# Three crossings of a decoder layer: rows scaled block by block, turned into four banks, with weight splits held behind the last norm

## The chip, the cores and the metric

The kernel runs on one core of one Trainium2 chip. The metric is the device time of one execution in microseconds (us); lower is better. Engines are named as in the profile: PE is TensorE's matmul, PEld its weight load, DVE is VectorE, ACT is ScalarE, POOL is GpSimd, SP is SyncE, whose queue issues most DMAs.

## What is computed

One layer of a hybrid decoder: 512 tokens of 1024 channels, all in float32. Every sub-layer stands between two RMS norms, and its normed output is added to the residual stream `h`.

```
h = x + 0.5 * post(SwiGLU_1(pre(x)))                   # FFN, 1024 -> 2816 -> 1024
u = pre(h);  proj = u @ W_in                           # queries, keys, gates, conv input
h = h + post((sigmoid(ga)*(dsa(...) @ Wa) + sigmoid(gb)*(conv(...) @ Wb)) @ W_out)
h = h + post(CrossAttn(pre(h), rms(mem)))              # 4 heads, 256 memory rows
h = h + 0.5 * post(SwiGLU_2(pre(h)))

def rms_norm(x, g):
    return x * rsqrt(mean(x*x, axis=-1) + 1e-6) * g
```

The branch `dsa` picks at most 128 keys per query by a score of its own and attends to them.

## The kernel before, in words

**Precision.** Each float32 operand is split into a high part (rounded by ACT to the type that PE multiplies fast) and a low part (the rest, subtracted on DVE). A product is three matmuls: high by high, high by low, low by high (`mm3`, `by_token`). Weights are split as they are needed: `Weights.prepare` rounds on ACT (line 146) and subtracts on DVE (line 147). `fetch` keeps `PIECES_AHEAD = 8` pieces of 512 columns split ahead of the unit in use; a unit of eight row blocks is two pieces. The raw tiles that the DMAs fill are six; one is free again when its low part has been taken.

**Two layouts.** The residual `h` and the outputs of the sub-layers lie by tokens: four blocks `t` of 128 tokens, each 1024 channels wide in two column halves `c`. The input `u` of the next sub-layer lies by channels: eight row blocks `k` of 128 channels, 512 tokens wide. `u` is a pair of high and low tiles.

**A crossing** is the way from one to the other. There are three: from the first FFN to the mixer, from the mixer to the cross-attention, from the cross-attention to the second FFN. Each does the following.

- `end` or `only` takes the product of one part `(c, t)` from PSUM, squares it on ACT with a running sum and multiplies it by the post gain on DVE.
- `settle(t)` takes the first norm's factor (a root on ACT and four small DVE steps, `inverse`), adds the scaled output to `h[t]` in two DVE instructions, squares these two halves on ACT and takes the second norm's factor `y`.
- `turned` scales the rows of two blocks by `y` on ACT into tiles `hn` and transposes them on PE, 16 transposes for half of the tokens, into four PSUM banks `pu`. Blocks `k` and `k + 1` lie next to each other in one bank.
- `gain_in` reads each block from PSUM, times the pre gain, and splits it into `u`: on ACT the high part, on DVE the low part. In the last crossing ACT first writes the float32 value (`us`, line 487) and then rounds it, and DVE subtracts from that.

In the first and the last crossing (`crossing`) PE goes on meanwhile with `head`, four weight units that start the next product for half of the tokens as soon as that half of `u` is there. The parts go in the order t outside, c inside. The first turn, of blocks 0 and 1, stands in the last part, ahead of its matmuls in the first crossing and ahead of its last two row blocks in the last one. The second turn stands between the third and the fourth head of the first half. In the middle crossing the products for the memory's keys (`pkx`) and values (`pvx`) lie around the turns.

**Order.** A planner orders the instructions of each engine by priority with its own estimates of durations, and each engine runs them in that order. `early(n)` raises the priority of what is written in its block; in a crossing PE keeps the order of the program. PSUM has eight banks: six go round under the tag `acc`, two under `aux`; `pu` takes two of each. Temporaries, `hn` and the squares among them, share ten tiles under the tag `ev`.

Of the kernel before, what the change touches and what calls it, by code (L numbers as in the profile page):

```python
# [9 lines left out]
F32 = mybir.dt.float32  # L10
F32R = mybir.dt.float32r
AF = mybir.ActivationFunctionType
ALU = mybir.AluOpType
# [3 lines left out]
P = 128  # L17
D = 1024
T = 512
NM = 256  # L20
KD = D // P
# [15 lines left out]
BEHIND, AHEAD, EVAC = 700, 400, 40  # L37
# [182 lines left out]
def build(tc, a, out):  # L220
    nc = tc.nc
    vec, ten = InOrder(tc, nc.vector), InOrder(tc, nc.tensor)
    ctx = ExitStack()
    with ctx:
# [21 lines left out]
        def ev(shape, dt, name):  # L246
            return evp.tile(shape, dt, tag="ev", name=name, bufs=EV)

        def bank(name):
            return acc.tile([P, 512], F32, tag="acc", name=name, bufs=ACC)  # L250

        def xbank(name, other=False):
            if other:
                return bank(name)
            return aux.tile([P, 512], F32, tag="aux", name=name, bufs=8 - ACC)

        def early(offset):
            return tc.high_priority(offset=offset)
# [6 lines left out]
        ident = con.tile([P, P], F32, name="ident")  # L265
# [5 lines left out]
        order = []  # L271
# [50 lines left out]
        def mm3(ps, wh, wl, xh, xl, first, last):  # L322
            ten.matmul(ps, wh, xh, start=first, stop=False)
            ten.matmul(ps, wh, xl, start=False, stop=False)
            ten.matmul(ps, wl, xh, start=False, stop=last)

        def product(ps, w, x, sl=FULL, ks=None):

            for k in range(len(w)) if ks is None else ks:
                (wh, wl), t = w[k], x[k]  # L330
                mm3(ps, wh, wl, t[0][:, sl], t[1][:, sl], k == 0, k == len(w) - 1)
# [43 lines left out]
        def new_u():  # L375
            return [pair("u") for _ in range(KD)]


        h = []
# [14 lines left out]
        class Outputs:  # L394
# [66 lines left out]
                    vec.scalar_tensor_tensor(o, o, y, h[t][:, cols], op0=ALU.mult, op1=ALU.add)  # L461
                    nc.sync.dma_start(out[t][:, cols], o)

            def turned(self, ys, n):

                hs = []
                for i in range(2):
                    t, y = 2 * n + i, ys[i]
                    hs.append([ev([P, T], F32, "hn") for _ in COLS])
                    for c, cols in enumerate(COLS):  # L470
                        nc.scalar.activation(hs[i][c], h[t][:, cols], AF.Copy, scale=y)
                pu = [xbank("pu", k2 % 2 == 1).rearrange("p (k t) -> p k t", k=2) for k2 in range(4)]
                for k in range(KD):
                    for i in range(2):
                        ten.transpose(pu[k // 2][:, k % 2, i * P:(i + 1) * P],
                                      hs[i][k // 4][:, k % 4 * P:(k % 4 + 1) * P], ident)
                return pu

            def gain_in(self, pu, n, pre, u, us=None):

                for k in range(KD):
                    ps, g, (uh, ul) = pu[k // 2][:, k % 2], gain(pre, k), (v[:, HALVES[n]] for v in u[k])
                    if us is None:
                        split_scaled(uh, ul, ps, g)
                        continue
                    w = us[k][:, HALVES[n]]
                    nc.scalar.activation(w, ps, AF.Copy, scale=g)
                    split(uh, ul, w)

        def crossing(outputs, part, pre, head, us=None):  # L490


            u, half = new_u(), [None, None]
            ten.on = True

            def turn(n):
                with early(AHEAD):
                    half[n] = outputs.turned(ys[2 * n:], n)
                    outputs.gain_in(half[n], n, pre, u, us)

            ys = []
            for t in range(T // P):
                for c in range(2):
                    if (c, t) == (1, 3):
                        part(c, t, lambda: turn(0))
                    else:
                        part(c, t)
                with early(AHEAD):
                    ys.append(outputs.settle(t))
            for f in head[:-1]:  # L510
                f(u, HALVES[0])
            turn(1)
            head[-1](u, HALVES[0])
            for f in head:
                f(u, HALVES[1])
            ten.on = False
            return u

        def heads(n, cols=()):
            ps = [bank("ph") for _ in range(n)]  # L520
            held, cols = {}, dict(cols)

            def make(i):
                def f(u, sl):
                    m = cols.get(i, P)
                    if i not in held:
                        held[i] = ws.unit(m)
                    product(ps[i][:m, sl], held[i], u, sl=sl)
                return f
            return ps, [make(i) for i in range(n)]  # L530

# [94 lines left out]
        def wide_units(n):  # L626
            return [w for _ in range(n) for w in ws.unit(T)]
# [76 lines left out]
        u = new_u()  # L704
        total, rows = sums_and_rows()
        ph, head = heads(4)
# [10 lines left out]
        outputs = Outputs("ffn1_post_g", 0.5)  # L717
        us = [slot([P, 2, T], F32, "us") for _ in range(4)]
        part = ffn(outputs, u, us, ph, rows, "ffn1_pre_g")
        load_h(a["xt"])  # L720
        ph, head = heads(4, {1: 72})
        u = crossing(outputs, part, "mix_pre_g", head)


        cs = slot([P, 2, T], F32, "cs")
# [37 lines left out]
        ps = ph[0]  # L763
# [9 lines left out]
        ps = xbank("pvt")  # L773
# [112 lines left out]
        for c in range(4):  # L886
            pg, pc = bank("pgc"), bank("pci")
            product(pg, ws.unit(), u)
            t = ev([P, T], F32, "gc")
# [6 lines left out]
            for k in (1, 0):  # L896
                o = 2 - k
                vec.scalar_tensor_tensor(s[:, o:], z[:, :T - o], convw[:, c, k:k + 1], s[:, o:],
                                               op0=ALU.mult, op1=ALU.add)
# [58 lines left out]
        for i in range(KD):  # L958
            t = ev([P, T], F32, "mt")[:, :NM]
# [3 lines left out]
        outputs = Outputs("mix_post_g", 1.0)  # L963
        for c in range(2):
            w = wide_units(KD // 2)
            for t in range(T // P):
                ps = bank("pf")
# [6 lines left out]
        for f in range(KD):  # L974
            ps = bank("pkx")[:, :NM]
            product(ps, ws.unit(), mn, sl=slice(0, NM))
            split(kx[f][:, 0], kx[f][:, 1], ps)
        u = new_u()
        for n in range(2):
            outputs.gain_in(outputs.turned([outputs.settle(t) for t in (2 * n, 2 * n + 1)], n), n, "xattn_pre_g", u)  # L980
        vx = [[None, None], [None, None]]
        for c in range(2):
            pv = [bank("pvx") for _ in range(2)]
# [12 lines left out]
        qx, at = [], []  # L996
# [54 lines left out]
        for f in range(KD):  # L1051
            ps = bank("pq")
# [7 lines left out]
        outputs = Outputs("xattn_post_g", 1.0)  # L1060
        w, pf = [wide_units(KD // 2)], []

        def partly(ts, ks):
            for t in ts:
                if t == len(pf):
                    pf.append(bank("pf"))
                tok = slice(t * P, (t + 1) * P)
                for k in ks:
                    (wh, wl), (xh, xl) = w[0][k], at[k]
                    ten.matmul(pf[t], xh[:, tok], wh, start=k == 0, stop=False)  # L1070
                    ten.matmul(pf[t], xh[:, tok], wl, start=False, stop=False)
                    ten.matmul(pf[t], xl[:, tok], wh, start=False, stop=k == KD - 1)
# [9 lines left out]
        def part(c, t, between=None):  # L1082
            if c == 0:
                partly((t,), range(6, 8))
                outputs.only(0, t, pf[t])
                return
            if len(w) == 1:
                w.append(wide_units(KD // 2))
            ps = bank("pf")
            by_token(ps, t, at, w[1], between and 6, between)  # L1090
            outputs.only(1, t, ps)

        ph, head = heads(4)
        uss = [slot([P, 2, T], F32, "us") for _ in range(4)]
        u = crossing(outputs, part, "ffn2_pre_g", head, [uss[k // 2][:, k % 2] for k in range(KD)])


        for t in range(T // P):
            nc.sync.dma_start(out[t], h[t])
        outputs = Outputs("ffn2_post_g", 0.5)  # L1100
        part = ffn(outputs, u, uss, ph)
# [72 lines left out]
```

## Time and profile before

| what | value |
|---|---|
| median of 3 runs (lowest to highest) | 1243.95 us (1243.83 to 1244.94) |
| the profiled execution's own time | 1246.46 us |
| its span, first to last instruction | 1244.7 us |
| PE busy | 1216.2 us, 98% |
| DVE busy | 845.9 us, 68% |
| ACT busy | 571.7 us, 46% |
| POOL busy | 78.9 us, 6% |
| HBM | 149.24 MB read, 4.19 MB written |

The profile is of one execution. Times in its views count from the first instruction, so they are to be held against the span. An engine's busy time is the time in which at least one of its instructions runs. The granted clock is given as a share of TensorE's full clock of 2.4 GHz; 0.5 would be 1.2 GHz, and what lies between is a mean over the stretch.

### The profile page before, as it was taken

The page shows a single profiled execution, that of the slowest core. Times are in us where ns is not written, and L with a number is a line of the kernel's source. Part 1 is how long each engine was busy: PE and PEld are TensorE (multiplying, and loading weights), DVE is VectorE, ACT ScalarE, POOL GpSimd, SP SyncE. Part 2 cuts the span into 40 slices and gives each one's busy share as a digit, 9 for nine tenths or more (in the row PEclk, how much of TensorE's full clock was granted, in tenths as well). Part 3 has the DMA queues.
Part 4 walks back from the last instruction along what each step waited for, and adds up shares of the span by engine and source line. Part 5 has one row for each costly group of instructions (what it writes and reads, how often), then busy time and mean ns, then how long its engine had stood idle before and what let it go on. Part 6 is the DMA issues. An engine that isn't in the chain of part 4 may idle for free.

```text
span 1244.7 us, 18396 instructions
## 1 busy us (share of the span) xinstructions
PE 1216.2 (98%) x7108; PEld 1077.1 (87%) x7108; DVE 845.9 (68%) x1493; ACT 571.7 (46%) x997; POOL 78.9 (6%) x118
## 2 busy tenths in 40 slices
PE   7999999999989999999999999999899999999997
PEld 7889999999879888888887898888788999999985
DVE  6877587767766799964357784555527567777665
ACT  6444443434454365455453583444825434344241
POOL 0000101110002300000000000000000111100100
PEclk9999999999989999999999999999899999999999
DMA  8336657564704642222222444233323556755641
GB/s 306 85 102 154 152 152 176 155 167 120 273 14 122 175 131 73 80 91 80 68 68 85 169 137 151 68 119 103 119 68 86 138 156 164 169 153 140 150 136 68
DMA packets 60904, 159.36 MB, mean 128 GB/s; under 512 B 7824, under 2 KB 10384, under 8 KB 60816
## 3 DMA queue, kind: packets, MB, share of 16 engines
q1 hardware_dynamic: 50320, 139.04, 34.7%
q0 software_dynamic: 10496, 19.14, 9.2%
q8 instruction: 56, 0.92, 0.3%
q14 instruction: 32, 0.26, 0.1%
HBM read 149.24 MB, written 4.19 MB: 123 GB/s over the span
## 4 chain that ended last, share of the span: by engine, by line
PE 89%; DVE 5%; ACT 3%; issue 1%; DMA 1%; SPq 0%; DVEq 0%; ACTq 0%
PE q L213 26%; PE pf L213 24%; PE pgb L213 4%; PE ph L213 4%; PE pa L213 4%; PE pq L213 4%; PE pga L213 4%; PE pb L213 3%; PE pkx L213 2%; PE pvx L213 2%; PE pya L213 2%; PE pyb L213 1%; PE pqb L213 1%; PE pqa L213 1%; PE pu L213 1%
## 5 line engine op out<-in xcount | busy, mean ns | idle before, releaser
L147 DVE TENSOR_TENSOR wl<-wraw,wh 128x1024 fp32r<-128x1024 f32 x246 | 294.0, 1218 | 116.4 <-ACT wh L146 101.6
L146 ACT CAST wh<-wraw 128x1024 fp32r<-128x1024 f32 x246 | 250.9, 1048 | 111.3 <-DVE wraw L163 87.7
L213 PE MATMUL q<-rt,wh 128*128 128x256 f32 x768 | 139.7, 283 | 0.0
L213 PEld LDWEIGHTS q<-rt,wh 128*128 128x128 f32 x768 | 119.8, 192 | 0.0
L126 POOL DMA_DIRECT2D wraw<-in_up x64 | 55.3, 915 | 962.6 <-DMA wraw<-in_up 749.7
L213 PE MATMUL q<-rt,wl 128*128 128x256 f32 x384 | 108.9, 284 | 0.0
L213 PE MATMUL pf<-wh,hidh 128*128 128x512 f32 x256 | 100.6, 393 | 0.0
L213 PE MATMUL pf<-wl,hidh 128*128 128x512 f32 x256 | 100.4, 392 | 0.0
L213 PE MATMUL pf<-wh,hidl 128*128 128x512 f32 x256 | 100.1, 391 | 0.0
L213 DVE TENSOR_TENSOR o<-o,q 128x512 f32<-128x512 f32 (+1 forms) x128 | 67.6, 548 | 10.6 <-PE q L213 8.3
L213 PEld LDWEIGHTS q<-rt,wl 128*128 128x128 f32 x384 | 73.7, 192 | 0.3 <-DVE wl L147 0.3
L213 PE MATMUL q<-u,wh 128*128 128x256 f32 x384 | 70.4, 283 | 0.0
L213 PE MATMUL q<-r,wh 128*128 128x256 f32 x384 | 70.4, 283 | 0.0
L213 PEld LDWEIGHTS q<-u,wh 128*128 128x128 f32 x384 | 60.9, 192 | 1.3
L213 PEld LDWEIGHTS q<-r,wh 128*128 128x128 f32 x384 | 60.9, 192 | 1.2
L213 PE MATMUL pf<-wh,hid 128*128 128x512 f32 x192 | 60.5, 390 | 0.0
L213 PE MATMUL pgb<-u,wh 128*128 128x512 f32 x192 | 59.3, 389 | 0.0
L213 PEld LDWEIGHTS pf<-wh,hidl 128*128 128x128 f32 x256 | 48.4, 189 | 10.3
L213 DVE TENSOR_TENSOR f<-f,pf 128x512 f32<-128x512 f32 x48 | 32.8, 683 | 35.7 <-PE pf L213 35.6
L213 PEld LDWEIGHTS pf<-wh,hidh 128*128 128x128 f32 x256 | 48.6, 190 | 9.5
L213 PEld LDWEIGHTS pf<-wl,hidh 128*128 128x128 f32 x256 | 48.5, 189 | 9.1
L315 ACT CAST hidh<-o 128x1024 fp32r<-128x1024 f32 x16 | 16.8, 1051 | 85.9 <-DVE o L213 85.9
(265 smaller groups left out, 2735.7 us busy)
## 6 DMA issues: line engine op xcount, KB each, us to landing
wraw<-in_up SPq DMA_DIRECT2D x55, 512.0 KB, 5.2
wraw<-in_up SPq DMA_DIRECT2D x98, 256.0 KB, 4.6
wraw<-in_down SPq DMA_DIRECT2D x44, 512.0 KB, 4.4
wraw<-in_w_in SPq DMA_DIRECT2D x37, 512.0 KB, 4.4
wraw<-in_up POOLq DMA_DIRECT2D x64, 256.0 KB, 5.6
wraw<-in_w_out SPq DMA_DIRECT2D x8, 512.0 KB, 3.7
wraw<-in_w_k SPq DMA_DIRECT2D x8, 512.0 KB, 4.4
wraw<-in_w_v SPq DMA_DIRECT2D x8, 512.0 KB, 4.5
```

Of the source, the lines that this page charges most:

```text
L126: self.nc.gpsimd.dma_start(t[:, o:o + PIECE], src, accum_op=ALU.add)
L146: self.nc.scalar.copy(hi, src)
L147: self.nc.vector.tensor_sub(lo, src, f32(hi))
L213: ins = f(*args, **kwargs)
L315: nc.scalar.copy(dst_h, src)
```

## The change

- `settle` and the scaling of a block become one step, `normed(t)`: the rows of block `t` are scaled as soon as its second norm is known, column half 0 on ACT, column half 1 on DVE. `turned` only transposes.
- The eight row blocks go over the four banks in turn: block `k` lies in bank `k % 4`, so blocks `k` and `k + 4` share one.
- In the first and the last crossing, DVE instructions that are written in the block of the heads, among them the low parts of the weights that follow, are ordered behind the DVE half of the last `hn` (`tc.issue_after(last.ins)`).
- The second turn moves from ahead of the fourth head to behind its sixth row block.
- The order of the parts becomes an argument; the last crossing now takes `PARTS`, c outside and t inside, with the first turn in the last part as before.

```diff
-            def turned(self, ys, n):
-                hs = []
-                for i in range(2):
-                    t, y = 2 * n + i, ys[i]
-                    hs.append([ev([P, T], F32, "hn") for _ in COLS])
-                    for c, cols in enumerate(COLS):
-                        nc.scalar.activation(hs[i][c], h[t][:, cols], AF.Copy, scale=y)
-                pu = [xbank("pu", k2 % 2 == 1).rearrange("p (k t) -> p k t", k=2) for k2 in range(4)]
+            def normed(self, t):
+                y = self.settle(t)
+                hn = [ev([P, T], F32, "hn") for _ in COLS]
+                nc.scalar.activation(hn[0], h[t][:, COLS[0]], AF.Copy, scale=y)
+                return hn, vec.tensor_scalar(hn[1], h[t][:, COLS[1]], y, None, op0=ALU.mult)
+
+            def turned(self, hs):
+                pu = [xbank("pu", b % 2 == 1).rearrange("p (k t) -> p k t", k=2) for b in range(4)]
+                pu = [pu[k % 4][:, k // 4] for k in range(KD)]
                 for k in range(KD):
                     for i in range(2):
-                        ten.transpose(pu[k // 2][:, k % 2, i * P:(i + 1) * P], ...)
+                        ten.transpose(pu[k][:, i * P:(i + 1) * P], ...)
...
-            ys = []
-            for t in range(T // P):
-                for c in range(2):
-                    if (c, t) == (1, 3):
-                        part(c, t, lambda: turn(0))
-                    else:
-                        part(c, t)
-                with early(AHEAD):
-                    ys.append(outputs.settle(t))
-            for f in head[:-1]:
-                f(u, HALVES[0])
-            turn(1)
-            head[-1](u, HALVES[0])
-            for f in head:
-                f(u, HALVES[1])
+            for c, t in order:
+                part(c, t, (lambda: turn(0)) if (c, t) == order[-1] else None)
+                if c == 1:
+                    with early(AHEAD):
+                        x, last = outputs.normed(t)
+                        hs.append(x)
+            with tc.issue_after(last.ins):
+                for f in head[:-1]:
+                    f(u, HALVES[0])
+                head[-1](u, HALVES[0], 6, lambda: turn(1))
+                for f in head:
+                    f(u, HALVES[1])
...
-        u = crossing(outputs, part, "mix_pre_g", head)
+        u = crossing(outputs, part, [(c, t) for t in range(4) for c in range(2)], "mix_pre_g", head)
...
-            outputs.gain_in(outputs.turned([outputs.settle(t) for t in (2 * n, 2 * n + 1)], n), n, "xattn_pre_g", u)
+            hs = [outputs.normed(t)[0] for t in (2 * n, 2 * n + 1)]
+            outputs.gain_in(outputs.turned(hs), n, "xattn_pre_g", u)
...
-        u = crossing(outputs, part, "ffn2_pre_g", head, [uss[k // 2][:, k % 2] for k in range(KD)])
+        u = crossing(outputs, part, PARTS, "ffn2_pre_g", head, [uss[k // 2][:, k % 2] for k in range(KD)])
```

## Rows read from the trace of the kernel before

**Rows 1.** The page's first part: busy time, share, instructions.

```profile
PE 1216.2 (98%) x7108; PEld 1077.1 (87%) x7108; DVE 845.9 (68%) x1493; ACT 571.7 (46%) x997; POOL 78.9 (6%) x118
```

**Rows 2.** Stretches of the span: each engine's busy time, granted clock, DMA share, GB/s.

```profile
355.95:368.40 12.45, 9.06 (x35) 7.68 (x35) 5.70 (x17) 8.84 (x20) 0.00 (x0) 0.73 0.00 0
...
711.30:760.10 48.80, 48.56 (x322) 44.50 (x321) 35.54 (x75) 35.72 (x73) 0.00 (x0) 1.00 0.50 162
873.70:878.50 4.80, 3.52 (x23) 2.97 (x23) 1.85 (x7) 4.78 (x12) 0.00 (x0) 1.00 0.10 42
878.50:888.30 9.80, 9.62 (x73) 8.80 (x71) 8.27 (x17) 7.44 (x16) 0.00 (x0) 1.00 0.26 81
888.30:898.30 10.00, 6.20 (x30) 6.00 (x30) 4.33 (x14) 8.96 (x24) 1.77 (x2) 0.66 0.73 216
...
440.00:540.00 100.00, 99.19 (x457) 81.09 (x456) 98.16 (x241) 53.97 (x108) 0.00 (x0) 1.00 0.29 92
```

**Rows 3.** PE's instructions in order: start, us, shape, count, [idle before, releaser].

```profile
358.60 0.33 PE L213 MATMUL pu<-ident,hn 128*128 128x128 f32 x1 [2.49 <-ACT hn L471]
359.82 3.46 PE L213 MATMUL pu<-ident,hn 128*128 128x128 f32 x15 [0.90 <-ACT hn L471]
...
378.12 0.33 PE L213 MATMUL pu<-ident,hn 128*128 128x128 f32 x1 [0.98 <-ACT hn L471]
379.80 3.29 PE L213 MATMUL pu<-ident,hn 128*128 128x128 f32 x15 [1.35 <-ACT hn L471]
...
874.22 0.33 PE L213 MATMUL pu<-ident,hn 128*128 128x128 f32 x1 [0.39 <-ACT hn L471]
875.44 1.86 PE L213 MATMUL pu<-ident,hn 128*128 128x128 f32 x15 [0.90 <-ACT hn L471]
877.05 0.48 PE L213 MATMUL pf<-wh,at 128*128 128x512 f32 x1
...
890.81 0.33 PE L213 MATMUL pu<-ident,hn 128*128 128x128 f32 x1 [2.50 <-ACT hn L471]
892.44 3.46 PE L213 MATMUL pu<-ident,hn 128*128 128x128 f32 x15 [1.30 <-ACT hn L471]
```

**Rows 4.** DVE's instructions in order of time.

```profile
350.72 0.35 DVE L213 SCALAR_TENSOR_TENSOR stat<-stat 128x1 f32<-128x1 f32 x2
...
362.30 0.88 DVE L213 SCALAR_TENSOR_TENSOR u<-pu,gains,u 128x256 fp32r<-128x256 f32 x2 [0.54 <-ACT u L319]
...
860.93 0.35 DVE L213 SCALAR_TENSOR_TENSOR stat<-stat 128x1 f32<-128x1 f32 x2
...
898.56 0.76 DVE L213 TENSOR_TENSOR u<-us,u 128x256 fp32r<-128x256 f32 x2 [0.58 <-ACT u L315]
```

**Rows 5.** ACT's instructions in order of time.

```profile
854.83 0.60 ACT L424 ACTIVATE sq<-pf 128x512 f32<-128x512 f32 x1 [0.97 <-PE pf L213]
...
881.34 0.64 ACT L424 ACTIVATE sq<-pf 128x512 f32<-128x512 f32 x1
...
893.38 0.84 ACT L487 ACTIVATE us<-pu,gains 128x256 f32<-128x256 f32 x2 [0.38 <-PE pu L213]
```

**Rows 6.** The chain that ended last, merged: start, length, instructions of a piece.

```profile
319.37 32.68 PE pf L213 x144
...
383.09 14.32 PE ph L213 x120
...
895.90 15.46 PE ph L213 x120
```

**Rows 7.** Groups by line: count, busy, mean ns of one, idle before.

```profile
L471 ACT ACTIVATE hn<-h,stat 128x512 f32<-128x512 f32 x24 | 15.9, 713 | 0.5 <-DVE stat L213 0.5
...
L147 DVE TENSOR_TENSOR wl<-wraw,wh 128x1024 fp32r<-128x1024 f32 x246 | 294.0, 1218 | 116.4 <-ACT wh L146 101.6 <-issue 11.3 <-DMA wraw<-in_up 2.1
L146 ACT CAST wh<-wraw 128x1024 fp32r<-128x1024 f32 x246 | 250.9, 1048 | 111.3 <-DVE wraw L163 87.7 <-PE q L213 12.0 <-DMA wraw<-in_up 9.6
```

**Rows 8.** The selection's replacements, a group by line.

```profile
L213 DVE MATCH_REPLACE8 bias<-m,bias 128x256 f32<-128x256 f32 (+2 forms) x48 | 25.7, 538 | 0.0
```

More of the change, by code (lines that the diff above doesn't have):

```diff
@@ L462, in settle_last @@
                     nc.sync.dma_start(out[t][:, cols], o)
-            def turned(self, ys, n):
-                hs = []
-                for i in range(2):
-                    t, y = 2 * n + i, ys[i]
-                    hs.append([ev([P, T], F32, "hn") for _ in COLS])
-                    for c, cols in enumerate(COLS):
-                        nc.scalar.activation(hs[i][c], h[t][:, cols], AF.Copy, scale=y)
-                pu = [xbank("pu", k2 % 2 == 1).rearrange("p (k t) -> p k t", k=2) for k2 in range(4)]
+            def normed(self, t):
[6 more added lines that the diff above has]
+                pu = [pu[k % 4][:, k // 4] for k in range(KD)]
                 for k in range(KD):
                     for i in range(2):
-                        ten.transpose(pu[k // 2][:, k % 2, i * P:(i + 1) * P],
-                                      hs[i][k // 4][:, k % 4 * P:(k % 4 + 1) * P], ident)
+                        ten.transpose(pu[k][:, i * P:(i + 1) * P], hs[i][k // 4][:, k % 4 * P:(k % 4 + 1) * P], ident)
                 return pu
             def gain_in(self, pu, n, pre, u, us=None):
-                for k in range(KD):
-                    ps, g, (uh, ul) = pu[k // 2][:, k % 2], gain(pre, k), (v[:, HALVES[n]] for v in u[k])
+                for k, ps in enumerate(pu):
+                    g, (uh, ul) = gain(pre, k), (v[:, HALVES[n]] for v in u[k])
                     if us is None:
@@ L488, in gain_in, with crossing @@
                     split(uh, ul, w)
-        def crossing(outputs, part, pre, head, us=None):
-            u, half = new_u(), [None, None]
+        def crossing(outputs, part, order, pre, head, us=None):
+            u, hs = new_u(), []
             ten.on = True
@@ L497, in turn @@
                 with early(AHEAD):
-                    half[n] = outputs.turned(ys[2 * n:], n)
-                    outputs.gain_in(half[n], n, pre, u, us)
-            ys = []
-            for t in range(T // P):
-                for c in range(2):
-                    if (c, t) == (1, 3):
-                        part(c, t, lambda: turn(0))
-                    else:
-                        part(c, t)
-                with early(AHEAD):
-                    ys.append(outputs.settle(t))
-            for f in head[:-1]:
-                f(u, HALVES[0])
-            turn(1)
-            head[-1](u, HALVES[0])
-            for f in head:
-                f(u, HALVES[1])
+                    outputs.gain_in(outputs.turned(hs[2 * n:]), n, pre, u, us)
+            for c, t in order:
[10 more added lines that the diff above has]
+                    f(u, HALVES[1])
             ten.on = False
@@ L523, in make, with f @@
             def make(i):
-                def f(u, sl):
+                def f(u, sl, at=None, between=None):
                     m = cols.get(i, P)
@@ L527, in f @@
                         held[i] = ws.unit(m)
-                    product(ps[i][:m, sl], held[i], u, sl=sl)
+                    if at:
+                        product(ps[i][:m, sl], held[i], u, sl=sl, ks=range(at))
+                        between()
+                    product(ps[i][:m, sl], held[i], u, sl=sl, ks=range(at or 0, KD))
                 return f
```

## The prediction

> **What bounds the kernel now.** The page's table of busy time says that TensorE (PE) is the bound [rows 1]: all that can be won by a change of order is its idle time and the stretches in which it runs below its full clock. I then cut the span at the three crossings, where the tokens' rows are normalized, turned and split for the next product [rows 2]. The reader is to see that the three differ. In the second (711.30 to 760.10) PE is busy 48.56 of 48.80 us, because the memory's keys and values fill it. In the first, the stretch 355.95 to 368.40 has 9.06 of 12.45 us busy at a mean granted clock of 0.73. In the third, 888.30 to 898.30 has 6.20 of 10.00 at 0.66. Last I went to PE's instructions in order of time for the waits themselves [rows 3]. Each crossing turns two halves of the tokens, 16 transposes each. Ahead of them PE waits 2.49 + 0.90, 0.98 + 1.35, 0.39 + 0.90 and 2.50 + 1.30 us, always for the scaled rows hn on ScalarE (ACT). After the long waits the 15 transposes take 3.46 us, after the short one of the third crossing 1.86.
>
> What sets these waits: all four activations hn of a half are written where the half is turned, so they stand on ACT behind the settling of later blocks. The second half has a slower cause: on VectorE (DVE) the small steps of the last norm alternate with the low parts of weights, 1.2 us each [rows 7]. An undisturbed block goes from its square at 854.83 to its last small step (860.93 + 0.35) in 6.45 us, with two instructions of another block in its way. The last block of the third crossing starts its square at 881.34 and its last 15 transposes wait until 892.44 [rows 3 to 5].
>
> **The price of PE's work at full clock.** A 512-column matmul of the last slab is 32.68 / 144 = 0.227 us, a 256-column one of the heads 14.32 / 120 = 0.1193 [rows 6]. Fifteen transposes fill 875.44 to 877.05, so one is 0.107 and 16 are 1.72 [rows 3]. The heads are 4 x 2 x 24 = 192 matmuls, 22.91 us; three of them serve one row block, 0.358.
>
> **First crossing, part by part.** Scaling as each norm ends: hn of blocks 0 and 1 exist some 4 us before 355.95 (block 1's last small step is at 350.72 [rows 4]), so the first turn starts at 355.95 without its 3.39 us of waits. Half of each hn moves to DVE: 713 ns on ACT today, and on DVE I take 0.5, nearer to that than to nothing, since DVE's low part of twice the elements is 1.2 [rows 7]. The eight pieces of a crossing cost PE nothing but behind the last norm, where one counts, as today: PE's parts hide the others, and without that cover each pair would cost at most 0.7. The turn itself keeps the full clock (16 x 0.107), because PE now comes to it out of unbroken matmuls. The last part's 18 matmuls follow (4.08), then three heads (8.59), 18 matmuls of the fourth (2.15), the second turn (1.72), the other 6 (0.72) and the second halves of four heads (11.45). The sum is 1.72 + 4.08 + 22.91 + 1.72 = 30.43 us against 397.41 - 355.95 = 41.46 today [rows 6].
>
> Now what can still be late. The last norm starts when the last part ends (361.75), with 0.7 for the add and 6.45 for the chain; 0.7 for hn and up to one high part of a weight on ACT (1.05 [rows 7]) give 369.6 to 370.7. PE comes to the second turn at 355.95 + 1.72 + 4.08 + 8.59 + 2.15 = 372.49. So no wait is left; this is what the move by 18 matmuls gives, beside the splits that stay behind. Those four low parts (1.2 us each) now run from about 370 to 375 on DVE. They belong to the units after the heads, since eight pieces ahead are already split when the crossing begins, so PE needs them only after 386. Behind them on DVE wait the low parts of u, behind these the first head's second half; on SP the four loads into the freed raw tiles, then cos and sin, needed only by DVE's rotations.
>
> The rotation of banks: today two neighbouring blocks share a bank, and DVE's next pair of low parts (0.88) waits 0.54 for ACT each time [rows 4], 0.71 per block; inside a pair the second adds 0.40. With blocks over four banks I take 0.40 throughout. Against this, a bank is complete only when its second block is in it: the first read comes after the tenth transpose instead of the fourth, 1.07 us into the turn. The first low part of u would then be ready at 372.49 + 1.07 + 0.2 + 0.48 + 0.48 = 374.7, the last at 377.5, while PE wants the last at 374.93 + 7 x 0.358 = 377.4. That is a stall of 0.1; with the weight splits still in DVE's way to 375, or with the norm half a microsecond late, 1 to 3. I take 1.2, nearer the low end, because only the last split overlaps. **First crossing: 41.46 - 30.43 - 1.2 = 9.8 us won** (8.0 to 10.9).
>
> The wait by bank rests on the 0.54 us rows: ACT and DVE wait for each other though they read different columns. The Trainium skill (PSUM — Partial Sum Buffer, "PSUM bank collisions raise a hardware error") states the same and speaks against the new layout: readers are to be kept off a bank, not off an address, while PE writes it. By that rule the read waits for ten transposes; by addresses alone for two, and the four turns would begin their reads 0.86 us sooner, of which the two second turns would show, some 1.7 us in all.
>
> **Third crossing.** The new order of parts puts four short ones (6 matmuls each) first, then four of 24, and the first turn stands 6 matmuls from the end; PE's amount is the same: 1.72 + 1.36 + 22.91 + 1.72 = 27.71 us, from 873.70. Today the heads end at 895.90 + 15.46 = 911.36, 37.66 later [rows 6]. Here each block of u costs ACT two instructions, and ACT alone reads the banks, so their rotation wins nothing. From the first of them (893.38) to the last low part (898.56 + 0.76) it is 5.94 us [rows 4, 5], where PE wants 2.87. Today 24 matmuls of cover hide that in the second half; with 6 left it shows. First half: reads begin at 873.70 + 1.07 + 0.2, with block 2's hn on ACT in between (0.65), so u ends at 881.56; PE wants its last block at 876.78 + 2.51 = 879.29, a stall of 2.27. The first head ends at 881.92, the second turn starts at 889.80 (two heads and 18 matmuls later). The last norm, whose square still waits for u's casts until about 881.4, needs 7.2 to 8.2 us more, ends by 889.6, and is hidden, if only just. Second half: u ends at 889.80 + 1.27 + 5.94 = 897.01, PE wants it at 894.75: again 2.26. The heads end at 873.70 + 27.71 + 4.53 = 905.94. **Third crossing: 5.4 us won** (4 to 6.3).
>
> **Second crossing.** ACT and DVE get the same edits, but PE idles only 0.24 us there [rows 2] and u is used 15 us after it is ready: nothing. Without the cover of the values' products, a wait for ten transposes instead of four would cost 0.65 twice.
>
> **The sum.** 9.8 + 5.4 = 15.2 us. The profiled execution took 1246.46 us (span 1244.70), so it would take 1231.2; the median of the runs is 2.51 lower, so 1243.95 - 15.2 = 1228.7.
>
> **The rivals.** (a) The clock falls all the same. Transposes, then matmuls with gaps of 0.3 us per block, replace idle time; the rows show 0.73 and 0.66 for stretches with waits of 2.5 us and transposes, but 1.00 for 873.70 to 878.50 with 1.29 us of waits and the same 16 transposes, and 1.00 for 878.50 to 888.30 with small gaps [rows 2]. At half clock a second turn costs 1.6 more (3.46 against 1.86) and its next 6 to 8 triples some 2: twice 3.6, giving 1235.9. (b) The high parts of those weights, which nothing holds back on ACT, get into the last norm: four of them are 4.2 us [rows 7], of which at most one was counted. Three more (3.1) put hn at 373.8 in the first crossing and at 892.7 in the third; the low parts behind it then hold u back by another 3 in the first. PE waits 1.3 + 3 - 1.2 and 2.9 longer: 6.0 in all, 1234.7. (c) The first crossing's gain is swallowed later. From 440 to 540 DVE is busy 98.16 of 100 us [rows 2]; if it, not PE, set the pace there, 9.8 would be lost: 1238.5. With (a) in the third crossing as well, 1242. Against it: DVE's work there starts from the heads' results and moves with them, and PE is busy 99.19. (d) Slower: the planner puts the selection, 48 replacements of 0.54 us [rows 8] with as many searches of about the same length, some 51 us, in one piece ahead of the weight splits of that stretch. Eight pieces ahead cover four units, 4 x 24 x 0.227 = 21.8 us of PE, so a piece over 21.8 + 15.2 = 37 us decides; all 51 us of it would give 1228.7 + 51 - 21.8 = 1257.9. (e) The change does not do what it says: the ten shared buffers hold hn back (eight are hn's, squares need the others), and the first turns wait as now: 3.4 and 1.3 us less gain, 1233.4.
>
> **How the numbers follow.** Forecast 60 in 100, with 1226 to 1232 as its own range; (a) 13, (b) 8, (e) 7, (c) 5, (c) with (a) 3, (d) 4. The range goes from 1225.5, the low bounds of both stalls plus 1.5, to 1237, which takes in (a), (b) and (e). More than 0.2% (2.5 us, about what a measurement of this kernel can tell from no change) faster: 0.93 less a little for mixtures, 0.92. Within it: 0.04, from (c) with (a) and mixtures. Slower: 0.04.
>
> **What would show it.** First turns with no wait for hn and 1.9 us long; second turns 18 matmuls into the fourth head, no wait, clock 1.00; on DVE four low parts of weights directly behind the last hn; in the third crossing the first head of each half stretched from 2.9 to about 5 us, waiting for u; the first crossing's heads over at 397.41 - 9.8 = 387.6, the third's at 911.36 - 15.2 = 896.2, with unchanged work behind both. Wrong it would be by a clock below 1.00 behind the turns, by a wait for hn, or by PE gaps between 440 and 540 that grow beyond 0.81.

## The result and the profile after

The changed kernel took 1232.01 us (median of 4 runs, 1231.74 to 1232.19) against 1244.37 (4 runs, 1243.83 to 1244.94): a ratio of 0.9900, 95% interval 0.9883 to 0.9918, 12.4 us less. The forecast was 1228.7 with a range of 1225.5 to 1237. The profiled execution took 1232.19 us, span 1230.4, mean granted clock 0.997.

The page's busy times answer to [rows 1]:

```profile
PE 1211.4 (98%) x7108; PEld 1073.4 (87%) x7108; DVE 851.4 (69%) x1505; ACT 564.8 (46%) x985; POOL 78.9 (6%) x118
```

The same matmuls are counted busy for 4.8 us less. That goes with the low clock that is gone from the turns: the transposes behind the long waits alone took 4.6 us more than at full clock (3.46 + 3.29 + 3.46 against 3 x 1.86 [rows 3]). Twelve halves of hn have gone from ACT to DVE.

PE's waits by what ended them (us in all, times, longest). Before, this line led the list:

```profile
PE pu L213 <- ACT hn L471: 10.8, 8, 2.5
```

No wait for hn is left:

```profile
PE ph L213 <- ACT whl L146: 7.1, 1, 7.1
PE po L213 <- ACT pth L315: 0.7, 3, 0.3
PE ph L213 <- ACT u L315: 0.7, 2, 0.4
PE ps_stat L213 <- DVE rows L213: 0.6, 1, 0.6
PE ph L213 <- DVE u L213: 0.6, 1, 0.6
```

The third and the fifth line are new, and they are a part of the stalls for u that the prediction priced. The list does not show all of a stall: where PE gets on in small steps, as each piece of u comes, only the starts of its instructions tell it. PE's instructions in order of time, to set beside [rows 3]:

```profile
356.85 1.91 PE L213 MATMUL pu<-ident,hn 128*128 128x128 f32 x16
...
373.44 1.91 PE L213 MATMUL pu<-ident,hn 128*128 128x128 f32 x16
...
864.11 1.91 PE L213 MATMUL pu<-ident,hn 128*128 128x128 f32 x16
867.82 0.85 PE L213 MATMUL ph<-u,wh 128*128 128x256 f32 x2 [0.41 <-ACT u L315]
869.76 1.00 PE L213 MATMUL ph<-u,wh 128*128 128x256 f32 x2 [0.25 <-ACT u L315]
...
881.88 1.91 PE L213 MATMUL pu<-ident,hn 128*128 128x128 f32 x16
```

All four turns run through in 1.91 us, without a wait. The stretches that answer to [rows 2] (length, then busy time of PE, PEld, DVE, ACT and POOL, granted clock, DMA share, GB/s):

```profile
355.90:368.40 12.50, 12.50 (x87) 11.50 (x87) 10.79 (x35) 7.84 (x23) 0.00 (x0) 1.00 0.00 0
702.10:750.50 48.40, 48.40 (x321) 44.39 (x321) 37.23 (x80) 33.46 (x69) 0.00 (x0) 1.00 0.51 163
863.00:867.80 4.80, 4.41 (x28) 3.55 (x26) 3.33 (x13) 2.61 (x10) 0.00 (x0) 1.00 0.27 111
867.80:874.00 6.20, 5.67 (x25) 4.83 (x26) 4.12 (x12) 6.20 (x17) 0.00 (x0) 0.72 0.00 0
874.00:881.90 7.90, 7.90 (x69) 7.90 (x68) 6.01 (x17) 5.26 (x11) 0.00 (x0) 1.00 0.22 75
881.90:889.00 7.10, 6.92 (x49) 6.09 (x48) 5.03 (x10) 6.03 (x18) 0.00 (x0) 1.00 0.86 271
431.00:531.00 100.00, 99.16 (x456) 81.02 (x455) 98.47 (x241) 53.91 (x108) 0.00 (x0) 1.00 0.30 91
```

The first crossing has lost its gap and its low clock (9.06 of 12.45 us at 0.73 before). The third keeps one stretch, 867.80 to 874.00, in which ACT never rests, PE waits for u, and the clock is 0.72. The long stretch behind the first crossing swallowed nothing.

DVE's instructions in order of time around the first crossing's second turn:

```profile
371.09 0.49 DVE L213 TENSOR_SCALAR hn<-h,stat 128x512 f32<-128x512 f32 x1
371.50 4.80 DVE L147 TENSOR_TENSOR wl<-wraw,wh 128x1024 fp32r<-128x1024 f32 x4
376.21 3.22 DVE L213 SCALAR_TENSOR_TENSOR u<-pu,gains,u 128x256 fp32r<-128x256 f32 x8
```

The last hn, then the four low parts of weights, then u: the order foreseen. The stall behind it is the 0.6 us wait of the list above. ACT's instructions in order of time in the third crossing, first half:

```profile
865.32 0.63 ACT L424 ACTIVATE sq<-h 128x512 f32<-128x512 f32 x1 [2.19 <-DVE h L213]
...
865.95 0.62 ACT L424 ACTIVATE sq<-h 128x512 f32<-128x512 f32 x1
...
866.56 0.45 ACT L489 ACTIVATE us<-pu,gains 128x256 f32<-128x256 f32 x1
...
867.97 0.73 ACT L469 ACTIVATE hn<-h,stat 128x512 f32<-128x512 f32 x1
```

Two squares of block 2 stand ahead of the first read of the turned block, and block 2's hn comes in between. The prediction counted this hn, not the squares.

**Where the time went.** Between the crossings the work is the same, so each can be measured as the distance between two products outside it: the first from the first start of pf<-wh,hidh to the first of pgc<-u,wh, the third from the first start of pq<-u,wh to the last of pa<-u,wh. The start of pf tells how long the part ahead of all edits took. In us, for the profiled execution of each kernel of this study, with the median of its runs:

| kernel | start of pf | first crossing | third crossing | both | median |
|---|---|---|---|---|---|
| before | 161.6 | 269.2 | 188.8 | 458.0 | 1244.37 |
| before, again | 162.2 | 266.5 | 187.8 | 454.3 | 1243.08 |
| changed | 162.5 | 259.5 | 184.1 | 443.6 | 1232.01 |
| changed, again | 162.2 | 259.7 | 184.1 | 443.8 | 1232.21 |
| rows scaled where turned | 162.8 | 264.1 | 185.1 | 449.2 | 1235.04 |
| early rows alone | 163.1 | 263.9 | 186.9 | 450.8 | 1239.98 |
| splits not held | 162.1 | 259.9 | 185.5 | 445.4 | 1233.88 |
| banks as before | 162.5 | 260.1 | 182.8 | 442.9 | 1231.39 |
| second turn ahead | 161.2 | 260.3 | 182.9 | 443.2 | 1230.45 |
| four blocks outside | 162.5 | 259.4 | 182.6 | 442.0 | 1230.57 |
| splits behind u | 162.7 | 258.8 | 184.3 | 443.1 | 1231.48 |
| and a turn sooner | 162.1 | 259.0 | 183.2 | 442.2 | 1230.17 |
| all three | 161.6 | 259.0 | 181.7 | 440.7 | 1228.81 |
| all three, by bank | 162.5 | 259.2 | 181.8 | 441.0 | 1229.74 |

The start alone scatters by 1.9 us, though nothing ahead of it differs in the source; a difference of medians below that has to be looked for in the crossings.

### The profile page after: what moved, and what is told of

The parts are those of the page before. It is cut to its first block, busy times and chain, and to the rows that moved or that the text cites. A ratio compares the mean times of both kernels' runs of the same rounds, so it can differ in the third digit from the quotient of the medians.

```text
span 1230.4 us, 18394 instructions
## 1 busy us (share of the span) xinstructions
PE 1211.4 (98%) x7108; PEld 1073.4 (87%) x7108; DVE 851.4 (69%) x1505; ACT 564.8 (46%) x985; POOL 78.9 (6%) x118
## 4 chain that ended last, share of the span: by engine, by line
PE 86%; DVE 7%; ACT 3%; DMA 1%; issue 1%; SPq 0%; DVEq 0%; ACTq 0%
PE q L213 26%; PE pf L213 20%; PE ph L213 5%; PE pgb L213 4%; PE pa L213 4%; PE pq L213 4%; PE pga L213 4%; PE pb L213 4%; PE pkx L213 2%; PE pvx L213 2%; PE pya L213 2%; DVE f L213 2%; ACT sq L424 1%; PE pyb L213 1%; PE pqb L213 1%; PE pqa L213 1%
```

## The experiments

Each time goes with runs of the kernel before on the same chip: 1243.75 us for the kernel before again, the rows scaled where turned, the splits not held and the banks as before; 1243.63 for the second turn ahead, the four blocks outside, the splits behind u and the turn sooner; 1242.84 for the other four. The ratios are against these.

**The kernel before, again.** No edit. It asks whether the profiled execution, 2.51 us above the median, was longer by its waits or by its clock.

> The kernel before, unchanged, profiled again. Open is why the profiled executions lie 14.3 us apart (1246.46 and 1232.19) and the medians 12.4 (1244.37 and 1232.01). Theory 1: the waits ahead of the four turns are the same in each execution, but the time that PE then spends below its full clock differs, so that spans scatter by 1 to 3 us, the mean granted clock with them, and the profiled execution of before had more of it than most: a new profile has the same waits (10.8 us for hn in all, within 0.3), a span of 1242 to 1244.7, and the stretches behind the second turns end earlier where the span is shorter. Rival: the profiler itself costs the kernel before some 2 us in its waits: the new profiled execution is again at 1246 to 1247 and again 2 us above the median of its other runs.

1243.08 us (10 runs, 1241.71 to 1246.66), ratio 0.9998 (0.9987 to 1.0008); the profiled execution took 1242.87 at a mean clock of 0.995, where the earlier profile had 1246.46 at 0.991. PE's waits for hn and the turns in order of time:

```profile
PE pu L213 <- ACT hn L471: 10.8, 8, 2.5
```

```profile
360.36 2.70 PE L213 MATMUL pu<-ident,hn 128*128 128x128 f32 x15 [0.89 <-ACT hn L471]
...
379.18 1.86 PE L213 MATMUL pu<-ident,hn 128*128 128x128 f32 x15 [1.35 <-ACT hn L471]
...
889.89 3.15 PE L213 MATMUL pu<-ident,hn 128*128 128x128 f32 x15 [1.30 <-ACT hn L471]
```

The waits are those of [rows 3] to 0.02 us. What differs is the time that the same transposes took behind them: 2.70, 1.86 and 3.15 us against 3.46, 3.29 and 3.46. The kernel has no fixed price for its low clock: one of its runs at 1246.66 has 0.991, one at 1241.71 has 0.996.

**Rows scaled where they are turned.** The rest of the change stays.

```
 def normed(self, t):
-    hn = ...; return hn, vec.tensor_scalar(hn[1], ...)
+    return (t, self.settle(t)), self.stepped   # last small step
 def turned(self, ys):
+    for t, y in ys[:2]:   # both halves of hn, ACT and DVE
```

> The changed kernel, with the rows of a block scaled where they are turned, as before, half on ACT and half on DVE; all else as changed. Theory (the waits for hn ahead of the first turns were the larger part): the first turn of the first crossing waits 2 to 3.4 us again and loses another 2 to 3 to the clock, that of the third 0.5 to 1.3: 1236 to 1240. Rival (the banks, the held splits and the moved turn are what won): within 1 us of the changed kernel, 1231 to 1233.

1235.04 us (1233.83 to 1237.99), 0.9935 (0.9916 to 0.9954). Only the two first turns wait; the second ones, at 379.57 and 887.65, run through:

```profile
359.73 4.08 PE L213 MATMUL pu<-ident,hn 128*128 128x128 f32 x16 [2.49 <-ACT hn L474]
...
870.42 0.33 PE L213 MATMUL pu<-ident,hn 128*128 128x128 f32 x1 [1.31 <-ACT hn L474]
871.12 3.43 PE L213 MATMUL pu<-ident,hn 128*128 128x128 f32 x15 [0.38 <-ACT hn L474]
```

Early rows free the first turns. They are worth 3.0 us by the medians, less than expected; 5.6 in the crossings of the profiled execution, the longest of the four. Without them the rest of the change still wins 8.7 us on this chip (1243.75 - 1235.04).

**Early rows alone.** The kernel before, with normed as in the change and nothing else.

```
-    ys.append(outputs.settle(t))
+    ys.append(outputs.normed(t))   # hn scaled here, half on DVE
```

> The kernel before with one part of the change alone: a block's rows are scaled as its norm ends, half on ACT and half on DVE; banks, splits, second turn and order of parts as before. Theory: the first turns lose their waits (3.4 and 1.3 us) and what the clock took behind the first (about 3 us where it fell longest), and at the second turns the wait of the last block's two scalings shrinks by 1 us each; the splits still stand between the last norm's steps, so PE still waits for hn there, 1 to 2.5 us each: 1234 to 1238, about half to two thirds of the change's gain. Rival (the parts only work together): 1240 or more.

1239.98 us (8 runs, 1237.29 to 1240.83), 0.9971 (0.9961 to 0.9981): at the rival's edge. That is 2.9 us (1242.84 - 1239.98), where the whole change wins 10.6 on this chip (1242.84 - 1232.21, below). Now it is the second turns that wait:

```profile
357.39 1.91 PE L213 MATMUL pu<-ident,hn 128*128 128x128 f32 x16
...
375.94 2.71 PE L213 MATMUL pu<-ident,hn 128*128 128x128 f32 x15 [1.96 <-ACT hn L468]
...
869.46 1.91 PE L213 MATMUL pu<-ident,hn 128*128 128x128 f32 x16
...
887.56 2.36 PE L213 MATMUL pu<-ident,hn 128*128 128x128 f32 x15 [3.75 <-ACT hn L468]
```

PE comes to the second turns sooner, the last norm ends too late for them, and the longest wait grows from 2.5 to 3.75 us. The second turns' waits are 5.7 us in all, against 6.1 before (0.98 + 1.35 + 2.50 + 1.30). So the two parts of the change serve different turns.

**Splits not held.**

```
-with tc.issue_after(last.ins):
+with ExitStack():
```

> The changed kernel without the order that keeps DVE's work of the heads behind the last scaled rows; all else as changed. Theory: the low parts of four weights stand between the small steps of the last norm again, 3 to 4 us; 1.6 of them fit ahead of the second turn in the first crossing and 2.4 in the third, the rest is a wait for hn, and what is won by u's low parts no longer standing behind them is 1 us: 1233 to 1237. Rival: since the turn now stands 18 matmuls later, the splits fit under it, and freeing them only takes them out of u's way: 1230.5 to 1232.

1233.88 us (1233.36 to 1234.43), 0.9922 (0.9905 to 0.9939), 1.9 us over the changed kernel, as expected. DVE's instructions in order of time show the low parts back between the small steps, and the last hn at 373.92 instead of 371.09:

```profile
367.72 0.15 DVE L213 RECIPROCAL stat<-stat 128x1 f32<-128x1 f32 x1
367.79 1.20 DVE L147 TENSOR_TENSOR wl<-wraw,wh 128x1024 fp32r<-128x1024 f32 x1
368.92 0.15 DVE L213 TENSOR_TENSOR stat<-stat 128x1 f32<-128x1 f32 x1
...
373.92 0.49 DVE L213 TENSOR_SCALAR hn<-h,stat 128x512 f32<-128x512 f32 x1
```

PE then waits 1.43 and 1.59 us at the second turns.

**Banks as before.**

```
-pu = [pu[k % 4][:, k // 4] for k in range(KD)]
+pu = [pu[k // 2][:, k % 2] for k in range(KD)]
```

> The changed kernel with neighbouring row blocks in one bank again; all else as changed. Theory: in the first crossing ACT and DVE alternate on a bank, 0.71 us per row block in place of 0.40, which shows behind the second turn, where u is late: 1 to 2 us; in the third, where only ACT reads, it is 0 to -0.6, since the first read need not wait for the tenth transpose: 1232 to 1234. Rival: the rotation is what removes the stalls at all four turns: 1235 or more.

1231.39 us (1231.17 to 1232.05), 0.9903 (0.9888 to 0.9918): no difference to the changed kernel, where the theory wanted up to 2 us more and the rival still more. The table divides this nothing into two parts: the first crossing is 0.6 longer, the third 1.3 shorter. In the third crossing PE's second turn starts at 882.42, and ACT's first read of it is this one:

```profile
883.06 0.84 ACT L489 ACTIVATE us<-pu,gains 128x256 f32<-128x256 f32 x2
```

It comes 0.64 us behind the turn's start; in the changed kernel it is 883.17 - 881.88 = 1.29:

```profile
883.17 0.84 ACT L489 ACTIVATE us<-pu,gains 128x256 f32<-128x256 f32 x2 [1.05 <-PE pu L213]
```

The new layout helps where ACT and DVE both read the banks, and costs where ACT alone does and the first read is what counts. In the first crossing the theory had the place wrong: with the old layout PE falls behind u after the first turn, not after the second. The second turn starts 18.46 us behind the first (375.23 - 356.77) in place of 16.59, and most of these 1.9 us come back behind it, where u is now less late.

**Second turn ahead of the fourth head.** It undoes the move by 18 matmuls.

```
-head[-1](u, HALVES[0], 6, lambda: turn(1))
+turn(1)
+head[-1](u, HALVES[0])
```

> The changed kernel with the second turn ahead of the fourth head again, in both crossings; all else as changed. In the changed kernel's trace hn is whole at 371.82 in the first crossing and 879.47 in the third, and PE would come to the turn 18 matmuls (2.15 us) sooner, at 371.3 and 879.7. Theory: in the first crossing PE waits half a microsecond and then has 24 matmuls in place of 6 over the time in which u is late, 0 to 1 us better; in the third there is no wait, and of the two microseconds in which PE runs behind u most vanish, 1 to 2 us better: 1229.5 to 1231.5. Rival (the move is needed; without it PE waits for hn and the clock falls): 1233 to 1236.

1230.45 us (1230.32 to 1231.31), 0.9892 (0.9877 to 0.9907), within the theory's numbers. But the crossings make 0.4 us of it: the first is 0.8 longer, with a wait for hn of 0.4 at its second turn, the third 1.2 shorter, because 24 matmuls instead of 6 cover its u and the clock did not fall. The rest of the difference stands ahead of the edits, in a start 1.3 sooner. So the place of the turn is right for the first crossing and wrong for the third.

**Four blocks outside.** The third crossing walks its parts as the first does.

```
-u = crossing(outputs, part, PARTS, "ffn2_pre_g", ...)
+u = crossing(outputs, part, [(c, t) for t in range(4) for c in range(2)], ...)
```

> The changed kernel with the parts of the last crossing in the old order, t outside and c inside; all else as changed. Theory: PE's amount is the same and block 2's norm ends 1.4 us sooner, so its hn no longer stands among the first turn's reads on ACT: 0 to 0.7 us better, 1231 to 1232.3. Rival (the order c outside takes work from ACT and DVE ahead of the last norm): 1233 to 1235.

1230.57 us (1229.97 to 1231.67), 0.9892 (0.9877 to 0.9908), a little better than expected. From 863 to 905 PE is busy 41.46 us at 1.00, against 40.90 at 0.96 in the changed kernel. From first to second turn it takes 879.94 - 863.70 = 16.24 us against 17.77. The list of waits has none for u in the third crossing, but the stall is still there, as the starts show:

```profile
863.70 1.91 PE L213 MATMUL pu<-ident,hn 128*128 128x128 f32 x16
...
866.85 0.85 PE L213 MATMUL ph<-u,wh 128*128 128x256 f32 x2
...
868.18 0.85 PE L213 MATMUL ph<-u,wh 128*128 128x256 f32 x2
...
869.52 0.85 PE L213 MATMUL ph<-u,wh 128*128 128x256 f32 x2
...
879.94 1.91 PE L213 MATMUL pu<-ident,hn 128*128 128x128 f32 x16
```

Every two row blocks of the first head take 1.34 us, ACT's pace for two blocks of u, where their six matmuls need 0.72 at full clock.

**Splits behind u.** The low parts of weights are held until the last low part of u.

```
+ws.wait = True                        # no splits fetched ahead
 ... first half of the heads, done = [turn(1)]
+ws.wait = False
+with tc.issue_after(done[0].ins): ws.catch_up()
```

> The changed kernel, but the four low parts of weights that follow the last hn on DVE stand behind the last low part of u instead, as the next units are not fetched ahead until the second turn is written. Theory: in the first crossing u's low parts, which start at 376.21 behind 4.8 us of splits, start at about 375.2, and PE gets on 1 us sooner; in the third, where ACT sets the pace of u, nothing: 1230.5 to 1231.5. Rival (u waits for something else, ACT's casts or the banks): 1231.7 to 1232.5. A loss of over 1 us would say that the splits, now later, are late for the next products.

1231.48 us (1230.56 to 1232.18), 0.9898 (0.9883 to 0.9913). DVE's instructions show the new order:

```profile
375.45 3.23 DVE L222 SCALAR_TENSOR_TENSOR u<-pu,gains,u 128x256 fp32r<-128x256 f32 x8 [3.69 <-ACT u L328]
378.59 4.62 DVE L148 TENSOR_TENSOR wl<-wraw,wh 128x1024 fp32r<-128x1024 f32 x4
```

From 356 to 390 PE is now busy 34.00 of 34 us (33.44 before this edit), and the first crossing is 0.7 shorter. The third is not: its second turn comes sooner (17.17 us behind the first), but behind it only two matmuls of the later product pa fill PE's stall, where the changed kernel has six.

**And a turn sooner.** The same, with the second turn after 3 row blocks of the fourth head in the first crossing and after 1 in the third.

```
-def crossing(outputs, part, order, pre, head, us=None):
+def crossing(outputs, part, order, pre, head, at, us=None):
-head[-1](u, HALVES[0], 6, ...)
+head[-1](u, HALVES[0], at, ...)     # at = 3, then 1
```

> As the run with the splits last, and the second turn stands behind the fourth head's third row block in the first crossing and behind its first in the third. Theory: the turns come at 372.4 and 880.1, behind hn, so there is no wait, and 15 and 21 matmuls in place of 6 hide u's lateness; against the changed kernel 1 to 1.5 us in the first and 1.5 to 2 in the third: 1228.5 to 1230. Rival (PE's stalls behind u are filled by the planner with matmuls of the next product anyway): 1230.5 to 1232.

1230.17 us (1229.60 to 1231.59), 0.9889 (0.9870 to 0.9908), just over the expected band. The third crossing gains 1.1 over the run above.

**The changed kernel, again.** No edit.

> The changed kernel, unchanged, beside the three that follow. It gives what the earlier runs lacked, its time on the same chip as the versions compared with it: 1231.4 to 1232.4, a spread below 1.5 us, where the kernel before has 4 to 5, since no wait of over 1 us is left that lets the clock fall for long. Rival: the spread is the chip's and not the waits': 3 us or more here too.

1232.21 us (4 runs, 1231.12 to 1233.28), 0.9910 (0.9890 to 0.9930), clocks 0.996 to 0.998. On this chip the change wins 10.6 us, not 12.4, as the kernel before takes 1242.84. Its executions spread over 2.2 us, less than the kernel before's 5 but more than expected. Its profile shows the same stretch of 0.72 in the third crossing (867.50 to 873.70).

**All three.** Splits behind u, the turns sooner, four blocks outside.

> The splits behind u's last low part, the second turn behind the third row block of the fourth head in the first crossing and behind the first in the third, and the parts of the third crossing with t outside. Theory: the gains of the single runs against the changed kernel lie at different places and add up in part, 1.4 from the order, 1.5 from the turns: 1228 to 1229.7. Rival (they all remove the same stall behind u in the third crossing): 1230 to 1231.

1228.81 us (4 runs, 1228.67 to 1229.04), 0.9882 (0.9867 to 0.9897), as expected: the best version, below both kernels. The list of waits has none for hn or u in the crossings, the clock of the run is 0.999. In the third crossing's first half PE still goes at ACT's pace: two row blocks start at 866.32, the next two at 867.66. The turns, and ACT's first read behind the last of them:

```profile
355.90 1.91 PE L222 MATMUL pu<-ident,hn 128*128 128x128 f32 x16
...
371.41 1.91 PE L222 MATMUL pu<-ident,hn 128*128 128x128 f32 x16
...
863.17 1.91 PE L222 MATMUL pu<-ident,hn 128*128 128x128 f32 x16
...
877.61 1.91 PE L222 MATMUL pu<-ident,hn 128*128 128x128 f32 x16
```

```profile
878.90 0.84 ACT L498 ACTIVATE us<-pu,gains 128x256 f32<-128x256 f32 x2 [1.73 <-PE pu L222]
```

**All three, by bank.** The same, with the transposes in the order of the banks, so that a bank is complete after four.

```
-for k in range(KD):
+for k in (0, 4, 1, 5, 2, 6, 3, 7):
```

> As the run together, with the 16 transposes of a turn in the order of the banks (blocks 0, 4, 1, 5 and so on), so that a bank is complete after four transposes and not after ten. Theory: ACT's first read of a turn comes 0.64 us sooner, as the reads wait for the whole bank, and where PE runs behind u this is won at up to three turns: 0.5 to 1.5 us better than together. Rival (the reads wait for their own block only, or u is never late any more): within 0.4 us of it.

1229.74 us (1229.36 to 1229.95), 0.9889 (0.9874 to 0.9904), 0.9 more than the one above; the theory's gain did not come. At the third crossing's second turn the reads do start sooner:

```profile
878.86 1.91 PE L222 MATMUL pu<-ident,hn 128*128 128x128 f32 x16
```

```profile
879.50 0.84 ACT L498 ACTIVATE us<-pu,gains 128x256 f32<-128x256 f32 x2 [1.09 <-PE pu L222]
```

That is 0.64 us behind the turn's start against 878.90 - 877.61 = 1.29. PE then runs behind this turn without a gap, but only some 0.3 us of stall was left there to win. At the third crossing's first turn the first read is no sooner (2.19 us behind the turn's start, 1.97 in the run above): a square of another block stands ahead of it on ACT, not the bank. Both crossings together differ by 0.3 us. The 0.9 is the start of pf, ahead of any edit, for which I have no cause.

## Why the prediction was right, and what it missed

**The waits and their cause: right.** 10.8 us of waits for hn became none, and the two experiments that each undo one half put them back at just the turns that the prediction gave to that half: the rows' place at the first turns, the weight splits at the second.

**The first crossing: right in size against its own profile.** It won 9.7 us where 9.8 was forecast. The second turn starts 16.59 us behind the first, against 16.54 in the prediction's sum (372.49 - 355.95). The heads were to be over at 387.6; they end at 388.66, from a start 0.9 later. The stall, taken at 1.2, was 0.6 in the waits, 0.7 by the experiment that removes it and about 1.0 by the starts, and its cause was the one named, the low parts of weights ahead of u.

**The third crossing: right in kind, 0.7 too high.** It won 4.7, not 5.4. From the first turn to the second PE's work takes 13.82 us at full clock (1.72 + 1.36 + 8.59 + 2.15). With the stall of 2.27 for u the prediction had 16.10; the changed kernel took 17.77. Two things were missed. ACT's first read came 2.45 us behind the turn's start (866.56 - 864.11) instead of 1.27, since two squares of block 2 stood ahead of it: 1.2 of the 1.7 us. The rest is the clock: rival (a) came true in this one place. The changed kernel's two profiles have 0.72 there and 17.7 to 17.8 us from turn to turn. Four variants with the same two waits, or a shorter first one (splits not held, banks as before, second turn ahead, splits behind u), kept 1.00. In the three of these whose second turn waits for no hn it is 17.17, 17.38 and 17.17, with 2.15 us added to the one that turns 18 matmuls earlier. So the low clock costs about 0.5 us, and block 2's work ahead of u about 1 (17.2 against 16.24 with four blocks outside).

That these 16.24 are near the 16.10 of the sum is in part luck: there the first read came 0.7 later than in the sum, and the hn of 0.65 that the sum puts among the reads stood ahead of them. Behind the second turn the prediction erred to the other side. The heads end 16.41 us behind its start (898.29 - 881.88), of which six matmuls of the later product pa, which run among the heads' own from 886.84, take 1.36: 15.05 for the heads, where the sum has 16.14.

**The term that failed: "the median of the runs is 2.51 lower".** The sum of 15.2 was made against the profiled execution, and profile against profile the two crossings won 458.0 - 443.6 = 14.4, the part between them 0.7: 15.1. But the 2.51 us by which that profile stood above its median was carried over to the changed kernel as if it were fixed. Run again, the kernel before shows what it was: time at a low clock behind the same waits, more of it in that execution than in most. The change removes that time with the waits, so it can't be subtracted a second time. The changed profile stands 0.18 above its own median. That is 2.3 of the 3.3 us between 1228.7 and 1232.0; most of the rest is the start, 0.9 us later in this execution (161.6 to 162.5), where the two kernels do not differ. Against the second profile of the kernel before, the crossings win 454.3 - 443.6 = 10.7, near the 10.6 by which the medians differ where both kernels ran again. One bound of the range does not follow from its own terms: 1228.7 less 1.1 and 0.9 for the low bounds of the stalls and 1.5 is 1225.2, not 1225.5.

**The edits taken one by one.** Early rows and held splits are worth 3.0 and 1.9 us when only one is taken away. The rows alone win 2.9, and all but the rows 8.7: together 11.6, against 10.6 to 12.4 for the whole. So the rows and the rest about add up; most of the gain lies in the rest, and no run has the held splits or the moved turn alone, so how it divides is not shown. With the splits not held the second turns wait 3.0 us in all, and with the turn not moved 0.4, against 6.1 before: of these two the held splits do more there. The rotation of banks was priced as 0.40 instead of 0.71 us for each row block in the first crossing and as nothing in the third; it is worth 0.6 in the one (1.9 up to the second turn) and costs 1.3 in the other, of which the later first read is 0.65 and the rest the clock. The wait by bank stood as a rule beside the 0.54 us rows, and the runs bear it out: with the same transposes, ACT's first read came at 0.64 us when a bank was complete after four and at 1.29 when after ten, and the 0.65 between them is six transposes of 0.107. The Trainium skill (PSUM — Partial Sum Buffer, "PSUM bank collisions raise a hardware error") asks for that guard by bank, not by address. By addresses both reads would have come after two transposes, at about 0.43 us (an estimate: 0.64 less two transposes).

**The rivals.** (b), splits on ACT in the last norm, (c), a gain swallowed between 440 and 540, (d), a late weight, and (e), hn held back by buffers, are all out: no wait for hn, and PE's gaps in the 100 us stretch are 0.84 against 0.81.

**Open.** Why the clock falls behind a pair of stalls in the third crossing of some kernels (the changed one, and the one with a turn sooner) and not in others with the same stalls; and whether the start's scatter belongs to the execution or to the kernel. All of it has come by the first product of pa (33.9 to 35.8 us): from there to pf it is 127.2 or 127.3 us in all fourteen profiles.

## What to carry to other kernels

Before a profile's span is set against the median, ask what made that execution longer: if it is low clock behind waits, it goes with the waits and is not an offset. Run a part of a change alone and also leave it out: only the two together tell whether the parts add up (here 2.9 and 8.7 us) or need each other. Do not take a stall for gone because the list of waits no longer has it: hold the distance between two starts against the work at full clock. A new layout of banks pays where two engines read a bank by turns, and costs where one engine reads alone and its first read is what counts: set it for each stage by itself.

## What the runs showed of the hardware

The granted clock behind waits of the same length is not the same from one execution to the next: 15 transposes behind a wait of 1.35 us took 3.29 us in one execution of the kernel before and 1.86 in another. Coming out of unbroken matmuls, the 16 transposes kept the full clock in every turn of the changed kernel, 1.91 us from the first's start to the last's end. On DVE a half of hn took 0.49 us, on ACT 0.73, so the half that moved became shorter as well.
